# A 2x2 average pool on one core: the next loads of a slot issued behind the scaling instead of behind the sums, and the last tile loaded on one queue

## Chip, cores, metric

One core of one Trainium2 chip. The metric is the device time of one execution in microseconds (us); quoted are medians of several executions, with the lowest and highest. The kernel before took 3103.57 us (3103.36 to 3104.26, 3 runs).

## The reference

```python
x = np.random.randn(32, 128, 256, 256).astype(np.float32)   # kernel_size 2, stride 2
output[:, :, i, j] = np.mean(x[:, :, 2*i:2*i+2, 2*j:2*j+2], axis=(2, 3))
```

1073.7 MB are read and 268.4 MB written; every output element is the sum of four inputs times 0.25.

## The kernel before

A row pair of the image is one output row. A tile is 32 such rows on each of 128 partitions, 64 KB a partition, 8.4 MB. There are two input slots (tile t uses slot t % 2) and two result buffers, each for a pair of tiles (4.2 MB). Each load comes in two halves of 64 partitions: SP (SyncE) issues the even partitions, ACT (ScalarE) the odd ones. VectorE (DVE) sums a tile in two instructions, ACT multiplies by 0.25 in place, GpSimd (POOL) stores a pair of tiles in one DMA. All engines run their own loop and meet in semaphores.

```python
def sums(it, dst):                    # DVE: rows, then columns
    dve.tensor_add(out=it[:, :, 0:w], in0=it[:, :, 0:w], in1=it[:, :, w:]).then_inc(halfway)
    take(dve, halfway)
    dve.tensor_add(out=dst, in0=it[:, :, 0:w:2], in1=it[:, :, 1:w:2]).then_inc(summed)

def next_load(b, *what):              # ACT
    take(act, summed)
    act.sem_inc(free[b])              # lets SP issue its half
    what[0](1, *what[1:])             # ACT's own half

def store(k, c):                      # GpSimd
    take(pool, scaled, 2)
    pool.dma_start(out=op[k], in_=both[c]...).then_inc(stored[c], 16)
...
with act.Fori(0, (pairs - 1) // 2) as i:
    for c in range(2):
        for b in range(2):
            next_load(b, load, 2 * i + (c + 1), b)
            scale(both[c][:, b], scaled)
```

`take` waits for a semaphore and takes its count off. The last, 128th tile comes in three parts (16, 8 and 8 rows), each on both queues, and is stored in three parts. The result buffer of a pair is given back to DVE when its store has landed.

Of the kernel before, what the change touches and what calls it, by code (L numbers as in the profile page):

```python
# [9 lines left out]
@with_exitstack  # L10
def kernel(
    ctx: ExitStack,
    tc: tile.TileContext,
    x: bass.AP,
    kernel_size: bass.AP,
    stride: bass.AP,
    out: bass.AP,
):
    nc = tc.nc
    P = nc.NUM_PARTITIONS  # L20

    n, c, h, w = x.shape
    k = int(kernel_size)
    s = int(stride)
    h_out = (h - k) // s + 1
    w_out = (w - k) // s + 1
    R = n * c * h_out
    units = R // P if R % P == 0 else 0


    if k == 2 and s == 2 and h % 2 == 0 and w == 256 and units >= 1024 and (units - 1) // 64 % 2 and (units - 1) // 32 % 2:
        _pool_2x2(ctx, tc, x, out, units)
    else:
        _generic_pool(ctx, tc, x, out, k, s, n, c, h, w, h_out, w_out)


TILE = 32


def _pool_2x2(ctx, tc, x, out, units):  # L40
    nc = tc.nc
    P = nc.NUM_PARTITIONS
    f32 = mybir.dt.float32
    w = x.shape[3]
    w_out = w // 2
    sp, act, dve, pool = nc.sync, nc.scalar, nc.vector, nc.gpsimd

    xv = x.rearrange("n c (ho a) w -> (n c ho) (a w)", a=2)
    ov = out.rearrange("n c ho wo -> (n c ho) wo")









    in_pool = ctx.enter_context(tc.tile_pool(name="inp", bufs=2))
    out_pool = ctx.enter_context(tc.tile_pool(name="outp", bufs=2))  # L60
    ins = [in_pool.tile([P, TILE, 2 * w], f32, name="in_tile") for _ in range(2)]
    both = [out_pool.tile([P, 2, TILE, w_out], f32, name="res") for _ in range(2)]
    res = [both[t // 2][:, t % 2] for t in range(4)]

    def sem(name):
        return ctx.enter_context(nc.semaphore(name))

    loaded, free, stored, emptied = [
        [sem(f"{n}{b}") for b in range(2)] for n in ("loaded", "free", "stored", "emptied")
    ]  # L70
    halfway, summed, scaled, held, done, tail = [
        sem(n) for n in ("halfway", "summed", "scaled", "held", "done", "tail")
    ]



    def take(engine, sem, n=1):
        engine.wait_ge(sem, n)
        engine.sem_inc(sem, -n)  # L79

    def block(r0, g):
        rows = slice(r0, r0 + g * P)
        return xv[rows].rearrange("(p g) f -> p g f", p=P), ov[rows].rearrange("(p g) f -> p g f", p=P)

    pairs, rest = divmod(units - TILE - 1, 2 * TILE)
    whole, rest = 2 * pairs + 1, rest + 1
    assert pairs % 2 and pairs >= 5 and rest <= TILE
    last = 2 * pairs * TILE * P
    xp = xv[0:last].rearrange("(k o p t g) f -> t o k p g f", o=2, t=2, p=P // 2, g=TILE)
    op = ov[0:last].rearrange("(k o p g) f -> k p o (g f)", o=2, p=P // 2, g=2 * TILE)  # L90
    parts, a = [], 0
    while a < rest:
        b = rest if rest - a <= 8 else a + (rest - a) // 2
        parts.append((a, b, sem(f"part{len(parts)}")))
        a = b

    def load(odd, k, b):
        (act if odd else sp).dma_start(out=ins[b][odd::2], in_=xp[b, odd][k]).then_inc(loaded[b], 16)

    def load_block(odd, dst, r0, g, landed):  # L100
        (act if odd else sp).dma_start(out=dst[odd::2], in_=block(r0, g)[0][odd::2]).then_inc(landed, 16)

    def load_last(odd):
        for a, b, part in parts:
            load_block(odd, ins[whole % 2][:, a:b], (whole * TILE + a) * P, b - a, part)

    def sums(it, dst):
        dve.tensor_add(out=it[:, :, 0:w], in0=it[:, :, 0:w], in1=it[:, :, w:]).then_inc(halfway)  # L108
        take(dve, halfway)
        dve.tensor_add(out=dst, in0=it[:, :, 0:w:2], in1=it[:, :, 1:w:2]).then_inc(summed)  # L110

    def tile_sums(t):
        if t % 2 == 0:
            take(dve, emptied[t // 2 % 2])
        take(dve, loaded[t % 2], 32)
        sums(ins[t % 2], res[t % 4])

    def scale(dst, sem):
        act.mul(out=dst, in_=dst, mul=0.25).then_inc(sem)  # L119

    def next_load(b, *what):

        take(act, summed)
        act.sem_inc(free[b])
        what[0](1, *what[1:])

    def store(k, c):
        take(pool, scaled, 2)
        pool.dma_start(out=op[k], in_=both[c].rearrange("p t g f -> p (t g f)")).then_inc(stored[c], 16)  # L129

    def emptied_by(c, landed):
        pool.wait_ge(stored[c], landed)
        pool.sem_inc(emptied[c])

    with tc.tile_critical():

        for b in range(2):
            load(0, 0, b)
        with sp.Fori(1, pairs) as k:
            for b in range(2):  # L140
                take(sp, free[b])
                load(0, k, b)
        take(sp, free[0])
        load_block(0, ins[0], last, TILE, loaded[0])
        take(sp, free[1])
        load_last(0)
        take(sp, held, 2)
        c = (pairs - 1) % 2
        sp.dma_start(out=op[pairs - 1], in_=both[c].rearrange("p t g f -> p (t g f)")).then_inc(tail, 16)


        for b in range(2):
            dve.sem_inc(emptied[b])
        with dve.Fori(0, whole // 4):
            for t in range(4):
                tile_sums(t)
        for t in range(whole - whole % 4, whole):
            tile_sums(t)
        it = ins[whole % 2]
        dst = ins[(whole + 1) % 2].rearrange("p g (s f) -> p (g s) f", s=4)[:, 0:TILE]  # L160
        for a, b, part in parts:
            take(dve, part, 32)
            sums(it[:, a:b], dst[:, a:b])


        for b in range(2):
            load(1, 0, b)
        with act.Fori(0, (pairs - 1) // 2) as i:
            for c in range(2):
                for b in range(2):  # L170
                    next_load(b, load, 2 * i + (c + 1), b)
                    scale(both[c][:, b], scaled)
        c = (pairs - 1) % 2
        next_load(0, load_block, ins[0], last, TILE, loaded[0])
        scale(both[c][:, 0], held)
        next_load(1, load_last)
        scale(both[c][:, 1], held)
        take(act, summed)
        scale(res[(whole - 1) % 4], done)
        take(act, done)  # L180
        act.dma_start(out=block(last, TILE)[1], in_=res[(whole - 1) % 4]).then_inc(tail, 16)
        for a, b, _ in parts:
            take(act, summed)
            scale(dst[:, a:b], done)
            take(act, done)
            act.dma_start(out=block((whole * TILE + a) * P, b - a)[1], in_=dst[:, a:b]).then_inc(tail, 16)


        store(0, 0)
        with pool.Fori(0, (pairs - 3) // 2) as i:  # L190
            for c in (1, 0):
                store(2 * i + (2 - c), c)
                emptied_by(1 - c, 16 * i + 16)
        store(pairs - 2, 1)
        for c in range(2):
            emptied_by(c, 16 * (pairs - 1) // 2)
        pool.drain()


        take(sp, tail, 16 * (len(parts) + 2))  # L200
# [95 lines left out]
```

## Time and profile before

| | before |
|---|---|
| time | 3103.57 us |
| DVE, ACT, POOL busy | 54%, 16%, 1% |
| bytes moved | 1342.2 MB, 434 GB/s from 100 to 3000 us |
| time without a packet, mean of 16 DMA engines | 6.9 us, all of it in the first 4 and the last 6 us |

The page lists DMA issues with the time from the issue to the last landing. Two rows of it matter later, the 127 half tiles on either queue:

```profile
in_tile<-in_x_dram ACTq DMA_DIRECT2D x127, 32.4
in_tile<-in_x_dram SPq DMA_DIRECT2D x127, 34.6
```

A half tile spends 32 to 35 us between issue and landing though a whole tile takes only 19.3 us of the engines at full rate: it stands in the queue behind the load ahead of it. The rest of the profile is read in the prediction.

### The profile page before, as it was taken

How to read it: one execution, taken by the hardware profiler on the slowest of the kernel's cores; microseconds unless marked ns; L12 is line 12 of the kernel's file. 1: busy time of each engine (PE TensorE's matmuls, PEld its weight loads, DVE VectorE, ACT ScalarE, POOL GpSimd, SP SyncE). 2: the span in 40 equal slices, each digit the busy share in tenths (PEclk: the TensorE clock that was granted, in tenths of full speed). 3: DMA queues.
4: the chain of work that ended last, by engine and by line, in shares of the span. 5: the costliest groups of instructions: out<-in, count | busy, mean ns of one | idle time of the engine just before them, and what ended most of it. 6: DMA issues, size and time to landing. Idle time of an engine off the chain costs nothing. (4 is left out here: it accounts for less than half of the span.)

```text
span 3102.0 us, 2728 instructions
## 1 busy us (share of the span) xinstructions
DVE 1679.3 (54%) x260; ACT 503.0 (16%) x161; POOL 38.0 (1%) x66
## 2 busy tenths in 40 slices
DVE  5555555555555555555555555555555555555555
ACT  1111112111111111111111111211112111121111
POOL 0000000000000000000000000000000000000000
DMA  9999999999999999999999999999999999999999
GB/s 419 433 434 437 433 433 428 438 433 432 433 440 428 434 441 433 427 433 439 432 433 438 428 438 431 434 434 432 435 436 433 439 432 433 434 431 434 434 433 406
DMA packets 30448, 1342.20 MB, mean 433 GB/s; under 512 B 5232, under 2 KB 5232, under 8 KB 5488
## 3 DMA queue, kind: packets, MB, share of 16 engines
q10 hardware_dynamic: 10976, 541.07, 40.3%
q1 hardware_dynamic: 10544, 541.07, 40.3%
q0 software_dynamic: 8928, 260.05, 19.4%
HBM read 1073.74 MB, written 268.44 MB: 433 GB/s over the span
## 5 line engine op out<-in xcount | busy, mean ns | idle before, releaser
L108 DVE TENSOR_TENSOR in_tile<-in_tile 128x8192 f32<-128x8192 f32 (+1 forms) x130 | 1112.9, 8561 | 1390.8 <-DVEq L79 1390.8
L119 ACT ACTIVATE res<-res 128x4096 f32<-128x4096 f32 x127 | 459.2, 3616 | 1967.0 <-ACTq L79 1943.3
L110 DVE TENSOR_TENSOR res<-in_tile 128x4096 f32<-128x4096 f32 x127 | 561.9, 4425 | 18.6
L119 ACT ACT_TABLE_LOAD x31 | 39.8, 1283 | 613.0 <-ACTq L79 613.0
L129 POOL DMA_DIRECT2D out_dram<-res x62 | 37.8, 610 | 2971.0 <-POOLq L79 2579.3
L119 ACT ACTIVATE in_tile<-in_tile 128x1024 f32<-128x1024 f32 (+1 forms) x3 | 4.0, 1341 | 7.3 <-ACTq L79 7.3
L110 DVE TENSOR_TENSOR in_tile<-in_tile 128x1024 f32<-128x1024 f32 (+1 forms) x3 | 4.7, 1581 | 0.4
L277 POOL MEMSET const-float32-0.0<- 128x1 f32 x1 | 0.1, 93 | 0.4 <-issue 0.4
L277 POOL MEMSET const-bfloat16-1.0<- 128x1 bf16 x1 | 0.1, 95 | 0.0
L277 POOL MEMSET const-float32-1.0<- 128x1 f32 x1 | 0.1, 93 | 0.0
L277 POOL MEMSET const-uint8-127<- 128x1 uint8 x1 | 0.1, 93 | 0.0
## 6 DMA issues: line engine op xcount, KB each, us to landing
out_dram<-res POOLq DMA_DIRECT2D x62, 4096.0 KB, 49.7
out_dram<-res SPq DMA_DIRECT2D x1, 4096.0 KB, 33.4
in_tile<-in_x_dram ACTq DMA_DIRECT2D x1, 2048.0 KB, 15.3
in_tile<-in_x_dram SPq DMA_DIRECT2D x1, 2048.0 KB, 18.1
in_tile<-in_x_dram ACTq DMA_DIRECT2D x2, 1024.0 KB, 23.0
in_tile<-in_x_dram SPq DMA_DIRECT2D x2, 1024.0 KB, 23.1
out_dram<-res ACTq DMA_DIRECT2D x1, 2048.0 KB, 16.1
in_tile<-in_x_dram ACTq DMA_DIRECT2D x127, 32.4
```

The lines of the kernel that those rows point to most:

```text
L108: dve.tensor_add(out=it[:, :, 0:w], in0=it[:, :, 0:w], in1=it[:, :, w:]).then_inc(halfway)
L110: dve.tensor_add(out=dst, in0=it[:, :, 0:w:2], in1=it[:, :, 1:w:2]).then_inc(summed)
L119: act.mul(out=dst, in_=dst, mul=0.25).then_inc(sem)
L129: pool.dma_start(out=op[k], in_=both[c].rearrange("p t g f -> p (t g f)")).then_inc(stored[c], 16)
L277: nc = _bacc.Bacc("TRN2", target_bir_lowering=False, num_devices=1)
```

## The change

Its intent, as the code suggests, is order: the store of a pair goes out after the next loads, which go out once the tile is done with altogether (SP, having issued its loads, gives the signal for the store); and the last tile needs fewer DMAs. The core of the diff:

```diff
-    def next_load(b, *what):
-        take(act, summed)
-        act.sem_inc(free[b])
-        what[0](1, *what[1:])
+    def scale_free(b, dst):
+        take(act, summed)
+        scale(dst, done)
+        take(act, done)
+        act.sem_inc(free[b])

     def store(k, c):
-        take(pool, scaled, 2)
+        take(pool, scaled)
...
             for b in range(2):
                 take(sp, free[b])
                 load(0, k, b)
+            sp.sem_inc(scaled)
...
-        load_last(0)
-        take(sp, held, 2)
+        for a, b, part in parts:
+            src = block((whole * TILE + a) * P, b - a)[0]
+            sp.dma_start(out=ins[whole % 2][:, a:b], in_=src).then_inc(part, 16)
...
-                    next_load(b, load, 2 * i + (c + 1), b)
-                    scale(both[c][:, b], scaled)
+                    scale_free(b, both[c][:, b])
+                    load(1, 2 * i + (c + 1), b)
```

The last tile's parts become 16 and 16 rows (`rest - a <= 16` in place of 8).

More of the change, by code (lines that the diff above doesn't have):

```diff
@@ L70, in _pool_2x2 @@
     ]
-    halfway, summed, scaled, held, done, tail = [
-        sem(n) for n in ("halfway", "summed", "scaled", "held", "done", "tail")
-    ]
+    halfway, summed, scaled, done, tail = [sem(n) for n in ("halfway", "summed", "scaled", "done", "tail")]
     def take(engine, sem, n=1):
@@ L92, in _pool_2x2 @@
     while a < rest:
-        b = rest if rest - a <= 8 else a + (rest - a) // 2
+        b = rest if rest - a <= 16 else a + (rest - a) // 2
         parts.append((a, b, sem(f"part{len(parts)}")))
@@ L101, in load_block @@
         (act if odd else sp).dma_start(out=dst[odd::2], in_=block(r0, g)[0][odd::2]).then_inc(landed, 16)
-    def load_last(odd):
-        for a, b, part in parts:
-            load_block(odd, ins[whole % 2][:, a:b], (whole * TILE + a) * P, b - a, part)
     def sums(it, dst):
@@ L161, in _pool_2x2 @@
         for a, b, part in parts:
-            take(dve, part, 32)
+            take(dve, part, 16)
             sums(it[:, a:b], dst[:, a:b])
@@ L170, in _pool_2x2 @@
                 for b in range(2):
-                    next_load(b, load, 2 * i + (c + 1), b)
-                    scale(both[c][:, b], scaled)
+                    scale_free(b, both[c][:, b])
+                    load(1, 2 * i + (c + 1), b)
         c = (pairs - 1) % 2
-        next_load(0, load_block, ins[0], last, TILE, loaded[0])
-        scale(both[c][:, 0], held)
-        next_load(1, load_last)
-        scale(both[c][:, 1], held)
+        scale_free(0, both[c][:, 0])
+        load_block(1, ins[0], last, TILE, loaded[0])
+        scale_free(1, both[c][:, 1])
         take(act, summed)
```

## The prediction

> **What bounds the kernel now.** I read the page of the profile first, its slices and its DMA part, because the two numbers to set side by side are the busy share of the compute engines and that of the DMA engines.
>
> ```profile
> span 3102.0 us, 2728 instructions
> DVE 1679.3 (54%) x260; ACT 503.0 (16%) x161; POOL 38.0 (1%) x66
> DMA  9999999999999999999999999999999999999999
> DMA packets 30448, 1342.20 MB, mean 433 GB/s; under 512 B 5232, under 2 KB 5232, under 8 KB 5488
> ```
>
> No compute engine is above 54%, the DMA row has no slice below 90%. A nine can hide 10% of idling, so I cut the run into a few stretches and read the last two columns, the mean busy share of the DMA engines and GB/s:
>
> ```profile
> core 0: us, DVE busy (x) ACT busy (x) POOL busy (x), PEclk, DMA share, GB/s
> 5.00:100.00 95.00, 51.90 (x8) 12.13 (x4) 0.72 (x1) 1.00 1.00 430
> 100.00:3000.00 2900.00, 1570.87 (x241) 472.42 (x150) 36.50 (x60) 1.00 1.00 434
> 3000.00:3097.00 97.00, 56.57 (x13) 18.49 (x7) 0.61 (x1) 1.00 1.00 430
> 3097.00:3099.00 2.00, 0.00 (x0) 0.00 (x0) 0.00 (x0) 1.00 0.35 143
> ```
>
> From 5 to 3097 us the share is 1.00. I also laid the trace's single packets in steps of 1 us: between 3 and 3097 us all 16 engines have a packet in every step. The kernel is a DMA stream of 1342.2 MB at 434 GB/s, which takes 3093 us, plus some 2.4 us until the first packet and some 6 us behind the last full step. Whatever only rearranges waits can cost nothing unless it makes some DMA engine run dry, and can gain at most those few edges. So the question is narrow: how long before it would run dry does a DMA engine get its next load, now and after the change? The timeline of two tiles shows it:
>
> ```profile
> start us, us, engine line op out<-in xcount [idle before <-releaser]
> 1504.59 0.50 ACTq L98 DMA_DIRECT2D in_tile<-in_x_dram  x1
> 1505.14 3.62 ACT L119 ACTIVATE res<-res 128x4096 f32<-128x4096 f32 x1 [20.29 <-ACTq L79]
> 1515.20 8.69 DVE L108 TENSOR_TENSOR in_tile<-in_tile 128x8192 f32<-128x8192 f32 x1 [10.92 <-DVEq L79]
> 1524.04 4.42 DVE L110 TENSOR_TENSOR res<-in_tile 128x4096 f32<-128x4096 f32 x1
> 1528.80 0.51 ACTq L98 DMA_DIRECT2D in_tile<-in_x_dram  x1
> 1529.35 3.62 ACT L119 ACTIVATE res<-res 128x4096 f32<-128x4096 f32 x1 [20.59 <-ACTq L79]
> 1540.58 8.69 DVE L108 TENSOR_TENSOR in_tile<-in_tile 128x8192 f32<-128x8192 f32 x1 [12.11 <-DVEq L79]
> ```
>
> A tile lands at 1515.2, is summed by 1528.46 (8.69 + 4.42 and 0.15 between), and its slot is loaded again from 1528.80. The other slot's load lands at 1540.5, 11.7 us after that issue. That 11.7 us is the time to the slowest of the DMA engines. The landing records (one per engine and half tile) give the fastest too: over all 126 issues in the middle, the first engine is through 7.5 us (slot 0) or 6.9 us (slot 1) after the other slot's load is issued, in the median; the tenth percentiles are 6.5 and 5.6.
>
> **What the Trainium skill says.** "DMA: Bandwidth & Descriptors", section "Where 436 GB/s comes from", puts the ceiling at 435.2 GB/s for 16 ports; the trace's 434 agrees, so there is no rate left to win. The same page, "Queues, rings and completion order", says each DMA engine goes round robin over the queues that have work, and takes each queue's work in order; the trace agrees (load packets of the two queues alternate, and a load issued at 37.3 us gets its first packet at 41.8, when the load ahead of it is through). Hence an engine idles only when all three queues are empty for it. Its section "Issuing engines are not separate DMA queues" says SP, ACT and GpSimd feed the same 16 engines and spreading over them saves issue time alone; so I give the one-queue load of the last tile no loss of rate (the trace has SP and ACT at 40.3% each and, near the end, one queue alone at 427 GB/s). "ScalarE: Activation LUTs", "What ACT_TABLE_LOAD costs", has 1283 ns for a table load; the trace has 31 of 1283 ns, one per pass of ACT's loop.
>
> **The change part by part.**
>
> *The later issue.* Removed from in front of the scaling: the issue of the loads. Put in front of the issue: one scaling (3.62 us, all 127 alike in the groups) and ACT's wait for its own result (about 0.05 us). ACT's own steps before an issue (free, address) stay at 0.3 us. So 3.7 us later in three tiles of four. In the fourth the table load comes after the wait for the sums in the built program, so 1.28 more: 5.0 us.
>
> *Does it show in the middle?* From an issue to its first packet I read 1.35 us (first issue at 1.06, first packet at 2.41), from the last packet to the landing about 0.55 us. Of the 7.5 and 6.9 us, 1.9 go there: the fastest engine has 5.6 or 5.0 us in hand. Take 3.7 off: 1.9 or 1.3 us remain; for the tile with a table load (slot 0) 0.6. Positive, and the store queue (19.4% of the DMA time) usually has packets waiting as well, though not always: its last data packet before 3058 goes at 3053. At the tenth percentile the margin is about zero. But an engine that runs dry lets the two laggards catch up. The spread between first and last landing is 2.4 us in the median and cannot be lost twice, since all engines carry equal bytes: the whole middle can lose some 2.4 us at most, and the slowest engine has over 4 us more in hand. I book 0.5 us.
>
> *The start.* There is no store and no spread yet. Slots 0 and 1 were loaded together, and the data packets of both are through between 41.75 and 42.36 us, on average at 42.05. Before:
>
> ```profile
> 37.29 0.52 ACTq L98 DMA_DIRECT2D in_tile<-in_x_dram  x1
> 37.84 1.28 ACT L119 ACT_TABLE_LOAD   x1 [37.84 <-ACTq L79]
> 39.13 3.62 ACT L119 ACTIVATE res<-res 128x4096 f32<-128x4096 f32 x1
> ```
>
> The load for slot 0 was issued 4.4 us before that and started without a gap. After: sums seen at 36.98, table load to 38.33, scaling to 41.96, issue at 42.3, first packet at 43.65. All engines idle for 43.65 - 42.05 = 1.6 us. The next one: slot 1 lands at 42.9, is summed at 56.3, scaled at 60.0, issued at 60.3, first packet at 61.7, and slot 0's load (19.3 us at 434 GB/s) runs to 63.0: no gap. So 1.6 us, once.
>
> *The last tile.* Its loads were issued at 3053.5, right after the sums of the tile in that slot; now at 3053.3 + 0.05 + 3.62 + 0.3 = 3057.3, first packet 3058.65. Most engines are through with the load ahead by about 3058.25 (landings from 3058.8): 0.4 us. All of it on SP's queue moves the same 8.4 MB in 19.3 us; three parts landed at 3071.6, 3076.5 and 3081.4, the two should land near 3072 and 3082. DVE is in one unbroken run from 3062.0 to 3089.2 there, and wants the second part at about 3082, so it waits little or not. The total of its work is the same. The final piece doubles: scaling 1.91 instead of 1.06 us, and the last store of 1 MB is issued 0.85 us later than that of 0.5 MB (3090.5). Since the engines are full until 3097 with stores that are ahead of it (4 MB, 2 MB, 1 MB), the bytes are through at the same time; I book 0.5 us for the end.
>
> *The stores.* The pair's store now waits for SP to have issued the loads. But the scaling starts earlier by the issue it no longer follows (0.7 us), and SP's issue takes about as long: no change. Its landing (49 to 50 us after issue) has some 6 us before DVE wants the buffer; no change.
>
> Sum: 1.6 + 0.5 + 0.4 + 0.5 = 3.0 us on 3103.57, so 3106.5 us.
>
> **The rivals.** (a) *The later issue opens a gap in every tile.* Then 3.7 us or part of it, times 127: 1 us a tile would give 3230, 0.5 us 3167. For it: the fastest engine's margin is thin, 0.6 to 1.9 us. Against it: the loop of one slot has room. From landing to first packet 13.3 + 3.7 + 0.3 + 1.35 = 18.7 us (20.0 with a table load), then the load with its part of the stores (10.5 MB) 24.2 us, together 42.9 to 44.2 us in a period of two tiles of 48.4 us (from the median distance of two stores). Only a lasting gap on single engines could break that, and it heals itself as above. (b) *The store queue takes over as the wait*: if stores came 4 us later, DVE would wait for a result buffer, whose 6 us would shrink to 2. Still zero, and I found no such delay. (c) *It is faster*: earlier stores or a better mix of transfers. Against it: 434 of 435 GB/s; the edges are some 8 us of idling in all, 0.3%; even half of it gained gives 3100. (d) *The last tile on one queue is slower*, if one queue could not keep the engines full: 10% on 19.3 us is 2 us, inside the range.
>
> **Range and chances.** The four terms are small and each is uncertain by its own size; the middle term is the one with a tail: zero to 2.4 us if healing works, some 5 more if the spread comes back a few times. Below, 3103.5 is a change that is hidden everywhere but for noise (the three runs before lie within 0.9 us). So 3103.5 to 3112. For 2% slower it would need 62 us, 0.5 us in every tile (rival a): 0.02. Faster by 2% isn't there to be had: 0.005.
>
> **What would show each step.** Right: in the windows the DMA share is 1.00 from 50 us on; a dip of about 1.6 us near 42 to 44 us in the packets; the median from issue to landing falls from 32.4 (ACT) and 34.6 us (SP) by about 4; ACT's issue stands behind its scaling; the store's distance from the sums is unchanged; last landings near 3072 and 3082 plus some 2 us of shift. Wrong: a DMA share of 0.98 or less in the middle, a slower rate at full share, DVE waiting for the second part of the last tile by over 1 us, or a time under 3102.

## The result

The changed kernel took 3132.52 us (3131.92 to 3134.80, 4 runs), 29 us more than the kernel before (3103.70 us with the fourth run that it had in this comparison) and outside the predicted range of 3103.5 to 3112. The ratio of the fast runs is 1.0094 (95% interval 1.0077 to 1.0112); ratios are the mean time of one kernel's fast runs over that of the other's of the same rounds, so not quite the ratio of the medians. It is within the 2% that the prediction called most likely, but the mechanism was missed. A run over 1.5% above the fastest of its kernel counts as slow and is left out of ratios; the two such runs below are named (their clock was 1.00 like all others).

The same rows of the page as for before:

```profile
span 3130.7 us, 2903 instructions
DVE 1679.1 (54%) x258; ACT 502.8 (16%) x160; POOL 38.0 (1%) x66
DMA packets 30112, 1342.20 MB, mean 429 GB/s; under 512 B 5152, under 2 KB 5152, under 8 KB 5152
in_tile<-in_x_dram ACTq DMA_DIRECT2D x127, 28.9
in_tile<-in_x_dram SPq DMA_DIRECT2D x127, 30.9
```

No compute engine got busier, the bytes are the same; the rate is lower, and the cushion from issue to landing has shrunk by 3.5 and 3.7 us, as foreseen. Where in the run is the rate lower? Stretches of the changed kernel, the last two columns being the DMA engines' busy share and GB/s:

```profile
core 0: us, DVE busy (x) ACT busy (x) POOL busy (x), PEclk, DMA share, GB/s
5.00:100.00 95.00, 47.97 (x7) 12.13 (x4) 0.72 (x1) 1.00 0.98 418
100.00:1250.00 1150.00, 620.99 (x96) 188.97 (x60) 14.60 (x24) 1.00 1.00 434
1250.00:2000.00 750.00, 406.62 (x62) 122.36 (x39) 9.13 (x15) 1.00 1.00 431
2000.00:3100.00 1100.00, 586.02 (x90) 171.94 (x54) 13.39 (x22) 1.00 1.00 425
```

The dip of the start is there (0.98). Then the first 1150 us run at full rate, and after that the rate sinks **at a busy share of 1.00**. The engines are not idle; their packets take longer. One pair of tiles from the later part, and the rate in the 13 us behind each of its two issues:

```profile
1925.11 0.50 ACTq L96 DMA_DIRECT2D in_tile<-in_x_dram  x1
1946.84 3.62 ACT L113 ACTIVATE res<-res 128x4096 f32<-128x4096 f32 x1 [22.04 <-ACTq L77]
1950.75 0.49 ACTq L96 DMA_DIRECT2D in_tile<-in_x_dram  x1
1952.07 0.61 POOL L125 DMA_DIRECT2D out_dram<-res  x1 [49.22 <-POOLq L77]
1955.41 8.69 DVE L102 TENSOR_TENSOR in_tile<-in_tile 128x8192 f32<-128x8192 f32 x1 [8.70 <-DVEq L77]
```

```profile
1926.00:1939.00 13.00, 5.55 (x1) 0.00 (x0) 0.00 (x0) 1.00 1.01 436
1951.00:1964.00 13.00, 8.59 (x1) 0.00 (x0) 0.61 (x1) 1.00 0.94 363
```

The issue of slot 0's load at 1925.11 costs nothing: 436 GB/s. That of slot 1's at 1950.75, 4.7 us before the other slot's tile is at DVE, is followed by 13 us at 363 GB/s. (A window books a packet where it starts, so a share can exceed 1 and a short window gains or loses bytes at its edges. With the bytes of each packet spread over its record, the two windows have 434 and 388 GB/s at busy shares of 1.00 and 0.99: the loss is there, but smaller than the line shows.)

To put a number on this I summed two things over all packets of a trace and divided by the 16 engines. **Idle**: time in which an engine has no packet. **Stretch**: what a packet's record takes beyond the usual time of its size (2.418 us for 64 KB, 1.213 for 32 KB, and so on) and a tolerance of 6 ns. These are sums of my own over the trace's packet records:

| profiled run | span | stretch | idle: first 100 us | middle | last 15 us |
|---|---|---|---|---|---|
| before | 3102.0 | 1.6 | 2.7 | 0.0 | 4.2 |
| changed | 3130.7 | 27.4 | 4.6 | 2.2 | 2.8 |

The spans differ by 28.7 us; stretch rose by 25.7 (27.36 less 1.63) and idle by 2.7 us, which is all of it but 0.3 us. And of the stretch in the middle, 22.8 us lie behind slot 1's issues and 0.2 us behind slot 0's.

### The profile page after: what moved, and what is told of

Its sections match the earlier page's. It is cut to its first block, busy times and chain, and to the rows that moved or that the text cites. A ratio compares the mean times of both kernels' runs of the same rounds, so it can differ in the third digit from the quotient of the medians.

```text
span 3130.7 us, 2903 instructions
## 1 busy us (share of the span) xinstructions
DVE 1679.1 (54%) x258; ACT 502.8 (16%) x160; POOL 38.0 (1%) x66
## 5 line engine op out<-in xcount | busy, mean ns | idle before, releaser
L102 DVE TENSOR_TENSOR in_tile<-in_tile 128x8192 f32<-128x8192 f32 x129 | 1112.7, 8626 | 1419.8 <-DVEq L77 1419.8
L113 ACT ACT_TABLE_LOAD x31 | 39.8, 1283 | 597.3 <-ACTq L77 597.3
```

The lines of the kernel that those rows point to most:

```text
L113: act.mul(out=dst, in_=dst, mul=0.25).then_inc(sem)
```

## The experiments

Each kernel was compared with runs of the kernel before on the same chip. "Margin" is the time from ACT's issue of a load to the first landing (of the first DMA engine) of the load ahead of it.

### Which part of the change

**The late issue alone** (the changed kernel with the last tile as before):

```diff
-        b = rest if rest - a <= 16 else a + (rest - a) // 2
+        b = rest if rest - a <= 8 else a + (rest - a) // 2
-        (the parts on SP)
+        load_last(0)          # and load_last(1) on ACT, behind scale_free(1, ...)
```

> The change's later issue and store relay, with the last tile loaded as before (three parts on both queues). Theory (the later issue costs the time: packets of loads that arrive at nearly empty queues take longer, above all from the middle of the run on): about 3131 us, 27 us over before, the stretched packets worth 20 to 27 us per engine. Rival (the last tile on one queue and the bigger last piece cost it): within 5 us of before.

Measured 3118.44 us (3108.86 to 3143.95, 4 runs), stretch 6.4 us in the profiled run, which was the fastest. **The last tile alone** (the kernel before with the last tile in two parts on SP; ACT only counts `free[1]` up):

> The kernel before with only the last tile changed: two parts, all on SP's queue. Theory (later issue is the cause): 3103 to 3106 us. Rival (the tail costs it): 3120 us or more.

Measured 3103.57 us (3103.34 to 3103.79), ratio 1.0000. The last tile costs nothing, the late issue everything. The number expected for the first of the two was too definite: its runs scatter over 35 us. **The changed kernel again**, for its scatter:

> The changed kernel itself once more, as a reference on this chip and for its scatter: the kernel with the late issue alone had runs from 3108.9 to 3144.0 us. Theory (the loss begins when the landing times of the DMA engines have drifted apart far enough, which differs from run to run): runs between 3108 and 3145 us, a scatter over 5 us. Rival (a fixed cost in each tile): 3132 us within 3 us.

Measured 3139.47, 3156.20 and 3175.29 us on another chip, and a fourth run of 3188.76 that counts as slow; the kernel before kept to 3103.5 to 3103.9 there. The ratio of the fast runs is 1.0172 (1.0126 to 1.0218). The changed kernel lost in both series of its runs, but the size of the loss is not a constant: fast runs of the changed kernel lie from 3131.9 to 3175.3 us. The range that was expected ended at 3145 and was too narrow.

### In proportion, or with a threshold

**Half of the delay** (the kernel before, issue behind the first half of the scaling):

```diff
-                    next_load(b, load, 2 * i + (c + 1), b)
-                    scale(both[c][:, b], scaled)
+                    take(act, summed)
+                    scale(both[c][:, b, 0 : TILE // 2], half)
+                    take(act, half)
+                    act.sem_inc(free[b])
+                    load(1, 2 * i + (c + 1), b)
+                    scale(both[c][:, b, TILE // 2 :], scaled)
```

> The kernel before, but the loads are issued after the first half of the scaling (1.91 us, and the table load in one tile of four), the second half after the issue. Theory (a threshold: nothing is lost while the fastest engine keeps over some 3 us of margin from issue to its landing; the margin before ends at 5.2 us): 3103 to 3107 us, stretched packets under 4 us. Rival (the loss goes with the delay): half of 28 us, about 3117 us.

Measured 3104.01 us (3103.76 to 3104.44), stretch 2.5 us. **A longer delay** (the changed kernel, and half of the tile multiplied by one ahead of the issue):

```diff
         take(act, done)
+        act.mul(out=dst[:, 0 : TILE // 2], in_=dst[:, 0 : TILE // 2], mul=1.0).then_inc(done)
+        take(act, done)
         act.sem_inc(free[b])
```

> The changed kernel with 1.9 us more between scaling and issue (half of the tile is multiplied by one again). Theory (threshold): the margin of slot 1, 3.6 us at the start of the changed kernel, is 1.7 here, so every tile pair loses from the start and not only from 1250 us on: 3160 us or more. Rival (loss proportional to the delay of 3.7 us): 28 times 5.6 over 3.7, about 3146 us, spread over time as in the changed kernel.

Measured 3203.37 us (3199.56 to 3213.60), stretch 85.8 us. Its windows lose from the start on:

```profile
100.00:1250.00 1150.00, 605.73 (x94) 269.55 (x104) 13.99 (x23) 1.00 1.00 421
1250.00:2000.00 750.00, 394.94 (x61) 174.74 (x67) 9.13 (x15) 1.00 1.00 420
2000.00:3000.00 1000.00, 524.64 (x81) 233.84 (x90) 12.18 (x20) 1.00 1.00 419
```

So 1.9 us of delay cost 0.4 us, 3.7 us cost 15 to 53 (medians of the late issue alone and of the changed kernel's fast runs on the second chip), 5.6 us cost 100: a threshold, not a price per us. It also takes away the thought that the second half of the run is slow for its place in memory; with less margin the first half is just as slow. The margins show the threshold. Here are 60 of slot 1's issues from each of two profiled runs, sorted by margin, and the mean stretch behind one of them:

| margin of slot 1's issue | changed | changed, longer delay |
|---|---|---|
| 0 to 1 us | 0.97 us (3 issues) | 1.51 us (6) |
| 1 to 2 us | 1.61 us (6) | 1.49 us (36) |
| 2 to 3 us | 0.72 us (13) | 0.87 us (16) |
| 3 to 4 us | 0.05 us (17) | 0.54 us (1) |
| 4 to 5 us | 0.00 us (21) | none |

(One more issue of the longer delay, at a margin below 0, had 1.51.) In the kernel before no margin was under 4.8 us, and none lost. Behind slot 0's issues the same small margins (32 of 60 between 0 and 4 us in the changed kernel, 52 with the longer delay) cost at most 0.06 us on average in any of these rows.

### Why slot 1 and not slot 0

Between the last packet of one pair's store and the first of the next, the store queue is empty. In the changed kernel that gap ends some 4 us behind GpSimd's issue, which follows slot 1's load by 1.3 us. In the later half of the run it begins 5 us ahead of GpSimd's issue for every second pair and at about that issue for the others; up to 2290 us nearly all the stretch is in the pairs with the long gap. Slot 0's issue falls into the middle of a store. **Slot 1 early, slot 0 late**, and **the mirror image** (in the second, `b == 0`; in both, the store is released by ACT's count of two scaled tiles):

```diff
+        if what and b == 1:           # before the scaling
+            act.sem_inc(free[b])
+            what[0](1, *what[1:])
         scale(dst, done)
         take(act, done)
-        act.sem_inc(free[b])
+        if not (what and b == 1):     # behind it
+            act.sem_inc(free[b])
+            ...
```

> The changed kernel, but slot 1's loads are issued at the sums again, slot 0's stay behind the scaling. Theory (a late issue costs only where the store queue is empty at the same time; that is after slot 1's issue, just ahead of a new pair's store, while slot 0's issue falls in the middle of a store): 3103 to 3109 us, stretched packets under 5 us per engine. Rival (thin margin alone costs, wherever it is): half of the loss, 3115 us or more.

> The mirror image: slot 0's loads at the sums, slot 1's behind the scaling. Theory: as slow as the changed kernel or slower, 3115 to 3160 us, since slot 0's load, issued earlier, is through earlier and leaves slot 1's issue with less margin. Rival (margin alone): the same as the run with slot 1 early.

Measured 3107.90 us (3107.30 to 3110.45), stretch 5.5 us, with slot 1 early; 3117.09, 3133.16 and 3146.55 us with slot 0 early, and a fourth run of 3168.39 that counts as slow. With slot 1 early, six of slot 0's 60 issues had a margin under 1 us, and none of the 1 us rows of its margins shows over 0.04 us of stretch a time. So in these runs a thin margin cost only where the store queue had nothing either; the runs without stores, below, put this to the test.

**Store each tile by itself**, so that the store queue would hardly be empty:

```diff
+        for t in range(2):
+            take(pool, scaled)
+            pool.dma_start(out=ot[t][k], in_=both[c][:, t]...).then_inc(stored[c], 16)
```

> The changed kernel, late issue and all, but each tile is stored by itself (2 MB, 16 KB runs, 126 less the last two tiles) once its loads are issued, so that the store queue is nearly never empty when a load arrives. Theory (empty store queue): stretched packets under 5 us per engine, 3103 to 3112 us, if the shorter runs do not slow the stores for another reason. Rival A (the start of a store is what stretches the packets): twice as many starts, so 3130 to 3160 us. Rival B (margin alone): 3115 us or more, like the changed kernel.

Measured 3336.80 us (3330.21 to 3340.31), and of no use for the question. The runs of a store are 16 KB instead of 32, so its packets are half as long while those of the loads stay at 64 KB, and a store of 2 MB took 49.7 us to land, as long as one of 4 MB. The result buffers came free too late: the engines idled for 180 us in the middle, and in the semaphore records many of DVE's waits end on the signal that a store has landed.

**No stores of pairs at all**, to see whether an empty store queue is enough or whether it is the start of a store that stretches the packets. Built on the kernel with half the delay; GpSimd only counts, DVE does not wait for result buffers; in the second, three quarters of the scaling stand ahead of the issue:

> Wrong on purpose: the kernel with the issue after half of the scaling, without the 62 stores of pairs (nothing gates the result buffers). A tile then lands about every 19.4 us, so the last landing comes about 3.8 us after an issue, 2.5 us with the table load, and no store ever starts. Theory A (an empty store queue is enough): packets stretched by 0.7 us per engine and more at many issues, over 20 us in all. Theory B (the start of a store is needed as well): stretched packets under 5 us in all; what is lost is idling at the issues with the table load alone.

> The same with three quarters of the scaling ahead of the issue (24 of 32 rows, 2.75 us, worked out from 1.91 us for 16 rows and 3.62 for 32): last landing 3.0 us after an issue, 1.7 with the table load. Theory A: over 60 us of stretched packets. Theory B: under 5 us of them, with idling of under 1 us at the issues with a table load.

Both gave wrong results. 2603.29 us with 53.4 us of stretch and 45 us of idle in the middle; 2633.04 us with 58.4 and 71 us. No pair's store starts in them (only the last one, near the end), so theory B falls: an empty store queue and a late load are enough. They also answer the question of this part. Without stores the first of these runs has 32.0 us of stretch behind slot 0's issues and 18.5 us behind slot 1's; at margins of 0 to 2 us slot 0 lost 0.65 us a time (40 issues), with stores at most 0.06 us at the same margins. Take the stores away, and slot 0 loses as well. The second missed the "over 60" of theory A by a little, and both idle far more than expected, so the lead that a load needs was still set too small. The windows of the first:

```profile
5.00:60.00 55.00, 26.23 (x4) 8.05 (x5) 0.00 (x0) 1.00 1.01 431
100.00:1250.00 1150.00, 748.68 (x115) 238.75 (x130) 0.00 (x0) 1.00 0.98 417
1250.00:2500.00 1250.00, 812.31 (x124) 255.98 (x139) 0.00 (x0) 1.00 0.98 416
```

### One half early

**SP's half at the sums, ACT's half behind the scaling**, and the reverse:

```diff
         take(act, summed)
+        act.sem_inc(free[b])          # SP early; in the reverse run ACT's own load stands here
         scale(dst, done)
         take(act, done)
-        act.sem_inc(free[b])          # in the reverse run this stays
+        act.sem_inc(scaled)           # SP early: ACT releases the store (reverse run: SP, as before)
```

> The changed kernel, but SP's half of each load is released at the sums; only ACT's half waits for the scaling. Theory (what costs is an engine without queued work): the half that is there early fills the time until the other comes, so 3103 to 3108 us. Rival (each queue by itself must be filled early): over 3115 us.

> The mirror image: ACT issues its half at the sums, SP's half is released after the scaling. Theory: 3103 to 3108 us as well. Rival (one queue is special; four fifths of the stretched time of the changed kernel is in ACT's packets): this one is good and the run with SP early is not, or the reverse.

With SP early 3102.05 us (3101.98 to 3102.07), stretch 1.5 us; with ACT early 3168.10 us (3133.99 to 3176.13), stretch 62.9 us. A late stretch of each, SP early first:

```profile
2000.00:3000.00 1000.00, 545.68 (x83) 161.09 (x51) 12.17 (x20) 1.00 1.00 434
2000.00:3000.00 1000.00, 529.23 (x82) 161.26 (x52) 12.16 (x20) 1.00 1.00 423
```

The first bears the theory out, half of the load in hand is cushion enough, and the second contradicts it. The two also differed in the store's time, 4.7 against 6.0 us behind the sums. Two runs swapped that, by releasing the store by ACT and by putting a small scaling ahead of the release, and a third took the way over SP out of the changed kernel:

> ACT's half issued at the sums, SP's half after the scaling, as in the slow one of the two half-early runs, but the pair's store is triggered by ACT as soon as it is scaled and not by way of SP: 1.3 us earlier. If the store's time decides: 3102 to 3110 us. If the queue decides: over 3125 us.

> SP's half released at the sums, ACT's half after the scaling, as in the fast one of the two, but the store is triggered only after ACT's issue and a small scaling of 512 columns (about 0.6 us), some 6.0 us after the sums instead of 4.7. If the store's time decides: over 3125 us. If the queue decides: 3102 to 3106 us.

> The changed kernel with the store triggered by ACT once both tiles are scaled, ahead of the issue of slot 1's loads and not by way of SP: some 0.7 us earlier, loads as late as in the changed kernel. If the store's time decides: 3103 to 3115 us. If the lateness of the loads decides: 3130 us or more, like the changed kernel.

Measured 3145.33 us (3143.15 to 3151.13), 3103.93 us (3103.49 to 3104.64) and 3163.14 us (3156.81 to 3165.08). The store's time does not decide; which queue is early does. The packets show one half of why. In the kernel before ACT's packets lead in every tile and its half is through about 3 us ahead of SP's. With SP early this order turns round: when SP's next half is issued, ACT's old half has 5.3 us of packets left on the engine that is furthest ahead, and when ACT's half is issued 4 us later, SP's stands ready. With ACT early, what SP's old half has left at that moment is 1.9 us behind slot 1's issues. So ACT's early half meets nearly empty queues all the same. Why the system settles in this state and not in the mirror image of the other, the runs do not show.

### Why the loss starts in mid-run

In the changed kernel the smallest margin of slot 1's issues is 3.6 us at the start and falls under 3 after 1250 us, while the distance between the first and the last landing of slot 0's tile grows from 0.9 to some 3 us. In the kernel before it grows too. **Levelling**: once, near 1490 us, slot 0's load waits until slot 1's has landed on all engines (DVE counts a semaphore up when it has taken that landing, ACT takes it ahead of its issue); and **its control**, with the same cut loops and the signal taken a tile later:

```diff
         take(act, done)
+        if even_out:
+            take(act, even)           # in the control: a tile later, behind sem_inc
         act.sem_inc(free[b])
```

> The changed kernel, in which one load of slot 0 (in the 31st pair, near 1480 us) waits until slot 1's load has landed on all DMA engines, which sets their landing times level. Theory (drift apart is what brings the margin under the threshold): an idle of 4 to 6 us there, then no stretched packets for some 700 us or longer, stretched packets under 8 us in all, 3108 to 3120 us. Rival (something else grows with time or place in memory): stretched packets in the second half as in the changed kernel, over 20 us, 3135 us or more.

> The control of the levelled run: the same cut loops, but the signal is taken one tile later, where it has long come, so nothing is levelled. If the levelling mattered: stretched packets after 1500 us of 15 us and more, and 3128 us or more. If the cut loops mattered: as in the levelled run, under 12 us after 1500 us and about 3118 to 3124 us.

Measured 3122.12 us (3121.22 to 3136.52), with 12.6 us of stretch after 1500 us; the control 3122.25 us (3110.33 to 3139.79), with 4.4 us. Both sums of stretch are of the profiled run, which for the control was its fastest. Neither set of numbers expected of the levelling was met; the control's median came out as it should if only the cut loops mattered, but its runs scatter over 29 us, and it ran on another chip. The trace shows that the edit did not level anything. Slot 0's load did wait (it went out at 1495.93, 0.3 us behind the last landing of slot 1's), but the engines idled for 0.15 us there instead of the expected 4 to 6, having a store to go on with, and that load landed over 4.0 us from the first engine to the last, the next one over 4.5. So this pair of runs says nothing on the drift. That the engines drift apart and so use up the margin fits the margins, but is not shown.

### A kernel that beats both

The run with SP's half early was faster than the kernel before, so it ran once more in five rounds:

> SP's half at the sums, ACT's half after the scaling, once more and in five rounds: 3102.0 us within 0.5 us, all runs under all runs of the kernel before, if the gain is real; 3103 to 3104 us if it belonged to that chip.

Measured 3102.09 us (3101.91 to 3102.30) beside 3103.55 us (3103.22 to 3103.63): all its runs lie under all of the other's, by 1.5 us or 0.05%. The ratio's interval, 0.9982 to 1.0009, does not exclude 1. The spans of the profiled runs differ by 1.8 us, and 1.5 of that lies at the end: the engines idle for 2.7 us in the last 15 us, before for 4.2. What does that was not tested.

## Why the prediction was wrong

**What bounds the kernel**: right. The stream of 1342.2 MB at 434 GB/s sets the time, and the loss is DMA time.

**The later issue**: right in size. The first one was worked out for 42.3 us and came at 42.39; the times from issue to landing fell by 3.5 and 3.7 us.

**The start**, 1.6 us: the idle of the first 100 us rose by 1.9 us. Right. **The last tile and the end**, 0.4 and 0.5 us: the last tile alone cost 0.0 us, and DVE did not wait for the second part. The idle of the last 15 us fell by 1.4 us in the changed kernel, where 0.5 more had been booked. Both small, as said, but too much. **The stores**: no change, as said; the issue stands 5.35 us behind the sums instead of 5.23.

**"Does it show in the middle?"**, 0.5 us and 2.4 at most: this is the step that failed, with 25.7 us more stretch and 2.2 of idle in its place. It rested on three statements.

1. "Hence an engine idles only when all three queues are empty for it." As a statement on idling it held. But I took idling for the only cost. Packets stretch from 2.4 to as much as 4.0 us while the engine counts as busy; 25.7 of the 28.7 us are that.
2. The lead needed was put at 1.9 us (1.35 from issue to first packet, 0.55 from last packet to landing). The first number was read at the very start, on idle engines. The loss begins under some 3 us of margin and is 1.5 us a time under 2. In the kernel with SP early, where ACT's half is issued 1.3 to 3.2 us before its own queue runs out and the engines are running, its first packet came 6.4 us (slot 1) to 8.5 us (slot 0) behind the issue, other queues' packets having gone first.
3. "An engine that runs dry lets the two laggards catch up ... cannot be lost twice." It was lost behind 22 of 60 issues of slot 1. In the windows all engines slow down together, the laggards too. The spread of 2.4 us that was to bound the loss is also that of slot 0's tiles alone; slot 1's land over 4.1 us in the median of the trace before.

That the store queue "usually has packets waiting as well, though not always" was in the prediction, with the right gap beside it. It was not followed to its end: the gap falls on the same issue each time, slot 1's, and that is where nearly all the loss lies. Of the rivals, (a) had the right place, the thin margin, and half a us per tile as its smaller figure; what came is about 0.2 us averaged over 127 tiles, and nothing at all in the first 40% of the run. The list of what would prove the prediction wrong did name what came: "a slower rate at full share". And the trace before held a warning that I had seen and passed over: around its first store, with one load in the queues, its rate fell to 327 GB/s from 66 to 68 us at a full share (bytes of each packet spread over its record). The store had been issued, but its first packet came at 69.2 us.

What stays open: what inside a DMA engine takes the longer time in a stretched packet, why SP's half and not ACT's has to be early, and what drives the margins down in mid-run and makes the time differ from 3109 to 3175 us between fast runs with the same late issue.

## What to carry to other kernels

In a kernel that keeps its DMA engines full, the lead of each issue is worth reading as a distribution, and a delay that leaves it above its threshold is free (1.9 us here cost 0.4), while a little more is not (3.7 us cost 15 to 53). Look for the moment when several queues run out together, since an issue that falls there is the one to move forward; here moving slot 1's issue, or SP's half of the loads, was enough; moving slot 0's, or ACT's half, was not. And read GB/s beside the busy share: from 2000 to 3100 us the share was 1.00 at 425 GB/s instead of 434, and the share alone would have hidden the loss.

## What the Trainium skill lacked or had wrong

- "DMA: Bandwidth & Descriptors", "Rules for kernel authors", advises issuing a DMA early to overlap it with compute, but says nothing on how early, nor that too late shows as longer packets and not as gaps. Here: under 3 us from issue to first landing of the load ahead, with the store queue empty, the 13 us behind such an issue had 388 GB/s instead of 434 at a busy share of 0.99 (bytes spread over the packets' records).
- The same page, "Specifications", has about 0.6 us to the first byte from SP or ACT and about 1 us from GpSimd. Here 1.35 us from ACT's first issue to the first packet on idle engines, and for the stores 3.7 us and more from GpSimd's issue to the first packet (3.9 us at 1952.07), with the engines busy on loads.
- The same page, "Issuing engines are not separate DMA queues" and the rules, says that spreading over queues only saves issue time, and that halves on two queues are not worth the trouble. For the rate that holds (the last tile on one queue cost 0.0 us). But issuing the two halves at different times held 434 GB/s where both late did not, and it mattered which queue was early: 3102 against 3168 us.
- The same page, "Queues, rings and completion order", has the engines go round robin by packets but doesn't say that packets differ in size and so weigh the shares. Here the records of loads are 64 KB and those of stores 32 KB; with stores cut to 16 KB runs, 2 MB took as long (49.7 us) as 4 MB before.
- "ScalarE: Activation LUTs", "What ACT_TABLE_LOAD costs": nothing lacking; all 31 took 1283 ns.
